# Two-layer hybrid block on one core: the retention branch's gated product goes through DRAM, attention's branch is projected last, and attention's outputs of two units share one PSUM bank

## The chip, the cores and the metric

The kernel runs on one core of one Trainium2 chip, in one launch. The metric is device time in microseconds. The kernel before the change took 2956.39 us (median of 3 runs, 2952.46 to 2957.08).

## The reference

Two layers work on 1024 latent tokens and 256 context tokens of width 1024. Each layer normalises, projects with one wide matrix, runs three token mixers on parts of the projection, gates each mixer's output with its own part of `z` and `g`, and adds the result back:

```
h = rms_norm(x) * (1 + scale) + shift
na, gla, ret, z, g = split(h @ w_in)
o[0] = neighbourhood_attention(na)      # windows of 8 x 16 on a 16 x 64 grid, plus all context tokens
o[1] = gated_linear_attention(gla)      # chunked, both directions
o[2] = retention(ret)                   # chunked, both directions
y = sum_i sigmoid(g[i]) * ((o[i] * silu(z[i])) @ w_branch[i])
x = x + gate * (y @ w_out)
```

`gate`, `shift` and `scale` come from a conditioning vector through `w_mod`. In the last layer only the latent tokens are put out.

## The kernel before

A Python driver writes out the whole order of the program ahead of time. It goes in slots: in each slot the stream of large matrix products (the GEMM stream, line L376) puts in two portions of 3072 moving columns, the workers are advanced twice, and the lane (`attention_lane`) once. `drv.mult` scales the portion, so a larger value spreads the mixers over more GEMM work. Every engine then runs its own list in order and waits on semaphores.

Each GEMM keeps a high and a low part of both operands in fp32r: a unit of `fm_unit` is 24 products of 128x128 weights with up to 512 tokens, a merge unit 12. Layer 0 has 1280 tokens in blocks of 512, 512 and 256, layer 1 has 1024 in two blocks. The stream's order in a layer is: projections for retention, GLA and attention, then 12 groups of `g`, then six groups of `z` (256 columns each, two units of 128 rows per block) in the order `Z_ORDER`, then the merge with branches in the order 2, 1, 0, then the product with `w_out`. `z` groups 0 and 1 belong to attention (branch 0), 2 and 3 to GLA (branch 1), 4 and 5 to retention (branch 2).

The lane runs retention, GLA and attention one after another beside that stream. In attention (`na`), a unit is 128 query tokens of two heads. Each unit is a worker: it loads `q`, `qz`, the bias `bt` and the values `vw`; scores on TensorE (`na_sw`, `na_sc`); softmax on VectorE and ScalarE (`soft1`, `soft2`); ten transposes (`na_ptw`, `na_ptc`) that are copied out as `PT`; then ten products into `na_o` (L1037), which ScalarE copies into `oN`. A new unit starts every three slots. There are 10 units for each of four head pairs in layer 0 and 8 in layer 1. When a head pair has written its outputs, `na_out` is counted up.

A `z` unit's evacuation (`z_evac`) loads the mixer's output `ot`, takes silu on ScalarE and VectorE (L1259, L1260), and multiplies. For branches 0 and 1 GpSimd multiplies (L1273) and SP stores the product to DRAM (`b<-st_z`); `load_b` reads it back in the merge as `rb` and splits it in high and low (L1312, L1313). For branch 2 the product is split at once into resident tiles `bact[2]` in the pool `E`. That pool takes the memory that attention frees, so the lane opens it only after attention has ended; then the lane computes `gate` (`mod_gate`, eight loads of `wt` with products `mod_ps`), and in layer 0 the next layer's shift and scale (`mod_ss`, 16 more).

`z` groups 0 and 1 wait until attention's outputs are written: `while d.get("na_out", 0) < 2 * (zi + 1) * per_pair: yield`. While the stream waits, slots go on without GEMM. All loads go through SP's queue, which starts a load only when its buffer is free and waits there in order. The 8 buffers of `stg` are shared by the evacuations.

Of the kernel before, what the change touches and what calls it, by code (L numbers as in the profile page):

```python
# [30 lines left out]
NCOL = (24, 32, 32, 24)  # L31
LD_LAG, LD_GAP = 3, 3
RT_M = 1.25
GL_M = (1.1, 1.1, 1.0)
GL_N = 13
NA_M1 = 0.7
BR_ORDER = (2, 1, 0)
Z_ORDER = (2, 3, 0, 1, 4, 5)


def _next_f(c):
# [67 lines left out]
def hybrid_kernel(ctx: ExitStack, tc: tile.TileContext, A: dict, out: bass.AP):  # L109
# [777 lines left out]
    def na(layer):  # L887
        d = L[layer]
        ntok, last = d["ntok"], d["last"]
        with tc.tile_pool(name=f"na{layer}", bufs=2) as pn:  # L890
# [21 lines left out]
            def load_v(p):  # L912
# [2 lines left out]
                dma(vcx, d["nv"][NLAT:NTOK, p * P:(p + 1) * P].rearrange("(c p) d -> p c d", p=P))  # L915
                yield

            def heads(p):
                (ks, kl), vcx = tiles["k", p], tiles["v", p]

# [55 lines left out]
                def load_vw(win):  # L976
                    half, j = win
                    cw = 4 * NCOL[j]
                    vw = pn.tile([P, 3, P], F32, tag="vw", name="vw", bufs=4)
                    dma(vw[0:cw], d["nv"][0:NLAT, p * P:(p + 1) * P].rearrange("(g c r) d -> (c r) g d", g=4, r=4)  # L980
                        [4 * COL0[j]:4 * COL0[j] + cw, half:half + 3, :])
                    return vw

                def evac_t(hd, pts, win, vw):
                    hs = slice(hd * 64, hd * 64 + 64)
                    ptw, ptc = pts
                    PT = pn.tile([P, 640], F32, tag="PT", name="PT", bufs=3)
                    ch = []
                    if win is not None:
                        half, j = win  # L990
                        cw = 4 * NCOL[j]
                        ve.tensor_copy(PT[0:cw, 0:384], ptw[0:cw, 0:384])
                        for i in range(3):
                            ch.append((vw[0:cw, i, hs], PT[0:cw, i * P:(i + 1) * P]))
                    sc.copy(PT[:, 384:640], ptc[:, 0:256])
                    for i in range(2):
                        ch.append((vcx[:, i, hs], PT[:, 384 + i * P:384 + (i + 1) * P]))
                    return ch

                def pair(qc, win, dst, after):  # L1000
                    q = pn.tile([P, 2, P], F32R, tag="q", name="q", bufs=3)
# [24 lines left out]
                    for _ in range(5):  # L1026
                        yield
                    ptc = psa("na_ptc", (P, 2, 2 * P))
                    ts = [transp(ps_[hd][0], win, ptc[:, hd]) for hd in range(2)]
                    yield  # L1030
                    cA, cB = [evac_t(hd, ts[hd], win, vw) for hd in range(2)]
                    yield
                    po = psa("na_o")
                    n = len(cA)
                    for i in range(n):
                        for hd, ch in ((0, cA), (1, cB)):
                            pe.matmul(po[64 * hd:64 * hd + 64, 0:P], ch[i][0], ch[i][1], start=i == 0, stop=i == n - 1)  # L1037
                    yield
                    pv = po[:, 0:P]
                    sc.copy(dst, pv.rearrange("d (r c) -> d r c", c=16) if win is not None else pv)  # L1040
                    if after is not None:
                        drv.defer(after)

                for half in range(2):
                    oN = stg("oN")
# [71 lines left out]
    def projections(layer):  # L1117
# [32 lines left out]
                    ga.done = True  # L1150
            gb.done = True

        def fm(g, ns, evac, by_block=False):
            need(g)
            units = [(m, t0, nn) for m in range(g.w // P) for t0, nn in blocks(ns[m])]
            if by_block:
                units.sort(key=lambda u: u[1])
            for m, t0, nn in units:
                yield from fm_unit(g, m, h, t0, nn, evac)
# [92 lines left out]
        def z_evac(zi):  # L1252
            def f(m, t0, nn, ps):
# [8 lines left out]
                def w():  # L1262
                    yield
                    yield
                    if br == 2:
                        bt = d["bact"][2]
                        ve.tensor_tensor(st[:, :nn], st[:, :nn], ot[:, :nn], op=ALU.mult)
                        hi, lo = bt.get(0, ro // P, t0, nn), bt.get(1, ro // P, t0, nn)
                        sc.copy(hi, st[:, :nn])
                        gp.tensor_tensor(lo, st[:, :nn], fv(hi), op=ALU.subtract)  # L1270
                        d["z_out"][t0] = d["z_out"].get(t0, 0) + 1
                    else:
                        gp.tensor_tensor(st[:, :nn], st[:, :nn], ot[:, :nn], op=ALU.mult)  # L1273
                        drv.defer(lambda: dma(d["b"][br][ro:ro + P, t0:t0 + nn], st[:, :nn]))
                drv.spawn(w())
            return f

        per_pair = 2 if last else 3
        d["z_out"] = {}
        for zi in Z_ORDER:  # L1280
            if zi < 2:
                while d.get("na_out", 0) < 2 * (zi + 1) * per_pair:
                    yield
            if zi == 0:
                d["want_E"] = True
            if zi == 4:
                while not d.get("E"):
                    yield
            yield from fm(G["z"][zi], [ntok] * 2, z_evac(zi), zi == 5)
        d["done"]["z"] = True  # L1290


    def merge(layer):
# [7 lines left out]
        def load_b(br):  # L1301
            pend = []
            for t0, nn in blocks(ntok) + [(None, 0)]:
                for k in range(4 if t0 is not None else 2):
                    if t0 is not None:
                        rb = stg("rb")
                        dma(rb[:, :nn], d["b"][br][k * P:(k + 1) * P, t0:t0 + nn])
                        pend.append((rb, k, t0, nn))
                    if len(pend) > 2 or t0 is None:
                        rb_, k_, u0, un = pend.pop(0)  # L1310
                        hi, lo = bact[br].get(0, k_, u0, un), bact[br].get(1, k_, u0, un)
                        sc.copy(hi, rb_[:, :un])  # L1312
                        ve.tensor_tensor(lo, rb_[:, :un], fv(hi), op=ALU.subtract)  # L1313
                    yield
                    yield

        def unit(g, br, bi, m, t0, nn):
            mt = m
# [32 lines left out]
            if end_unit():  # L1351
                yield

        w1 = drv.spawn(load_b(1))
        for bi, br in enumerate(BR_ORDER[:2]):
            if bi == 1:
                while not w1["done"]:
                    yield
                bact[0] = Act(f"bn{layer}", [Ep] * 5, 4, ntok)
                w1 = drv.spawn(load_b(0))  # L1360
            for mg in range(4):
                g = G["wb"][br][mg]
                need(g)
                for m in range(2):
                    for t0, nn in blocks(ntok):
                        while d["z_out"].get(t0, 0) < 4:
                            yield
# [46 lines left out]
    def attention_lane(layer):  # L1414
        d = L[layer]
        for key, fn in (("ret", retention), ("gla", gla), ("nqk", na)):
# [2 lines left out]
            yield  # L1419
            yield  # L1420
            yield from fn(layer)
        while not d.get("want_E"):
            yield
# [5 lines left out]
        d["E"] = E  # L1429
        gate_sb = pgb.tile([98, 256], F32, tag="gate_sb", name="gate_sb")  # L1430
        d["gbc"] = [pgb.tile([P, D], F32, tag=f"gb{v}", name=f"gb{v}") for v in range(1 if d["last"] else 2)]
        with tc.tile_pool(name=f"modw{layer}", bufs=2) as pmw, tc.tile_pool(name=f"modp{layer}", bufs=1) as pm:
# [221 lines left out]
```

## Time and profile before

| | |
|---|---|
| median of 3 runs | 2956.39 us |
| profiled execution | 2953.91 us |
| its span | 2952.1 us |
| TensorE busy | 2828.3 us (96% of the span) |
| VectorE, ScalarE, GpSimd busy | 1499.4, 1102.1, 1078.2 us |
| mean granted TensorE clock | 0.985 |

The profiled execution took 2.48 us less than the median. TensorE is busy nearly all the time, so what counts is where it idles. "Busy" of TensorE holds modelled ends of pipelined products; the idle time that the views give ahead of an instruction is the safer number.

### The profile page before, as it was taken

What the parts mean: (1) busy time and instruction counts of PE and PEld (TensorE: products, weight loads), DVE (VectorE), ACT (ScalarE), POOL (GpSimd) and SP (SyncE); (2) the same over time, 40 slices, a digit from 0 to 9 for tenths busy, and PEclk for the clock granted to TensorE, in tenths of its full rate; (3) what the DMA queues carried; (4) which work ended last, traced back from release to release, by engine and by line L of the source; (5) the groups of instructions that cost most, each with busy time, mean ns of one, the idle gap of its engine ahead of it and who ended that gap; (6) DMA issues with size and microseconds to landing.
All of it is one profiled execution on the core that took longest, in us unless ns stands there. A gap on an engine that the chain in (4) does not pass through costs nothing. (4 is left out here: it accounts for less than half of the span.)

```text
span 2952.1 us, 51923 instructions
## 1 busy us (share of the span) xinstructions
PE 2828.3 (96%) x19776; PEld 2433.6 (82%) x19776; DVE 1499.4 (51%) x3189; ACT 1102.1 (37%) x2569; POOL 1078.2 (37%) x1010
## 2 busy tenths in 40 slices
PE   7999999999999998899999999999999999879999
PEld 5999987788878887677899999987788788767889
DVE  5156567767514455424334346469766156562331
ACT  4133556554423434322113323456544244342110
POOL 4222125466411122043655332125665212204463
PEclk8999999999999999999999999999999999999999
DMA  6344433443244556467445354443433455645543
GB/s 239 107 142 130 139 105 111 115 133 104 92 144 135 170 151 189 125 199 233 136 126 149 104 166 119 132 121 109 145 111 111 148 160 182 181 125 164 183 129 108
DMA packets 390857, 418.69 MB, mean 142 GB/s; under 512 B 33788, under 2 KB 310284, under 8 KB 390608
## 3 DMA queue, kind: packets, MB, share of 16 engines
q1 hardware_dynamic: 353248, 361.59, 40.9%
q10 hardware_dynamic: 37360, 53.79, 5.2%
q8 instruction: 156, 2.56, 0.4%
q14 instruction: 93, 0.76, 0.1%
HBM read 302.72 MB, written 112.54 MB: 141 GB/s over the span
## 5 line engine op out<-in xcount | busy, mean ns | idle before, releaser
L376 PE MATMUL fm<-h,whi 128*128 128x512 f32 (+1 forms) x3936 | 922.6, 380 | 7.7 <-ACT st_g L1244 7.7
L345 POOL TENSOR_TENSOR wlo<-wraw,whi 128x512 fp32r<-128x512 f32 (+1 forms) x336 | 450.5, 1362 | 1000.4 <-ACT whi L342 892.0
L376 PEld LDWEIGHTS fm<-h,whi 128*128 128x128 f32 x3936 | 681.1, 190 | 157.8 <-issue 26.4
L376 PE MATMUL fm<-h,wlo 128*128 128x512 f32 (+1 forms) x1968 | 470.6, 374 | 0.0
L376 PEld LDWEIGHTS fm<-h,wlo 128*128 128x128 f32 x1968 | 339.8, 189 | 70.8 <-issue 8.7
L376 PE MATMUL tm<-whi,h 128*128 128x256 f32 (+1 forms) x2528 | 339.2, 284 | 2.0 <-ACT h L295 2.0
L376 PEld LDWEIGHTS tm<-whi,h 128*128 128x128 f32 x2528 | 318.2, 189 | 3.5 <-ACT h L295 2.7
L342 ACT CAST whi<-wraw 128x1024 fp32r<-128x1024 f32 (+1 forms) x168 | 175.8, 1048 | 268.4 <-PE tm L376 123.8
L376 PE MATMUL tm<-wlo,h 128*128 128x256 f32 (+1 forms) x1264 | 189.7, 286 | 0.0
L376 PEld LDWEIGHTS tm<-wlo,h 128*128 128x128 f32 x1264 | 166.6, 189 | 0.7 <-issue 0.2
L843 DVE TENSOR_TENSOR ek<-dd,kd 128x512 f32<-128x512 f32 x108 | 101.2, 937 | 93.4 <-ACT dd L833 93.2
L376 PE MATMUL tm<-whi,yy 128*128 128x256 f32 x1152 | 147.4, 280 | 0.0
L376 PEld LDWEIGHTS tm<-whi,yy 128*128 128x128 f32 x1152 | 140.7, 188 | 0.1
L1273 POOL TENSOR_TENSOR st_z<-st_z,ot 128x512 f32<-128x512 f32 (+1 forms) x40 | 48.2, 1209 | 253.1 <-DMA ot<-o 103.7
L798 POOL TENSOR_TENSOR dd<-Ac,ash 128x256 f32<-128x256 f32 x126 | 116.3, 923 | 51.5 <-ACT ash L785 31.0
L1260 DVE SCALAR_TENSOR_TENSOR st_z<-st_z,fm 128x512 f32<-128x512 f32 (+1 forms) x60 | 37.8, 633 | 174.4 <-ACT st_z L1259 172.5
L844 DVE SCALAR_TENSOR_TENSOR eq<-dd,g_col,qd 128x256 f32<-128x256 f32 x126 | 117.5, 933 | 13.1 <-ACT dd L833 13.0
L1244 ACT ACTIVATE st_g<-fm 128x512 f32<-128x512 f32 (+1 forms) x120 | 66.5, 557 | 144.0 <-PE fm L376 95.7
L1392 DVE TENSOR_TENSOR st_o<-tm,gb 128x256 f32<-128x256 f32 x72 | 30.5, 424 | 155.1 <-PE tm L376 152.0
L1334 DVE SCALAR_TENSOR_TENSOR gt<-gt,mg 128x512 f32<-128x512 f32 (+1 forms) x80 | 50.7, 634 | 112.5 <-PE mg L376 98.7
L833 ACT ACTIVATE dd<-dd 128x512 f32<-128x512 f32 x126 | 79.4, 635 | 75.3 <-POOL dd L799 73.1
L416 DVE COPY st_tm<-tm 128x256 f32<-128x256 f32 (+1 forms) x59 | 25.2, 428 | 161.5 <-PE tm L376 161.1
(1573 smaller groups left out, 4757.8 us busy)
## 6 DMA issues: line engine op xcount, KB each, us to landing
wraw<-in_w_in SPq DMA_DIRECT2D x104, 512.0 KB
wt<-in_w_mod SPq DMA_DIRECT2D x48, 512.0 KB
gd<-st_g ACTq DMA_DIRECT2D x96, 256.0 KB
gt<-gd SPq DMA_DIRECT2D x96, 256.0 KB
bt<-in_na_bm SPq DMA_DIRECT2D x32, 384.0 KB
ot<-o SPq DMA_DIRECT2D x48, 256.0 KB
wraw<-in_w_branch SPq DMA_DIRECT2D x24, 512.0 KB
v<-ret SPq DMA_DIRECT2D x38, 256.0 KB
```

Of the source, the lines that this page charges most:

```text
L342: sc.copy(hi[:, :, :w], raw[:, :, :w])
L345: gp.tensor_tensor(lo[:, ks, :w], raw[:, ks, :w], fv(hi[:, ks, :w]), op=ALU.subtract)
L376: pe.matmul(ps, a(k), b(k), start=i == 0, stop=i == tot - 1)
L798: gp.tensor_tensor(dv[:, :, Lh:], av[:, :, Lh:], rv, op=ALU.subtract)
L833: sc.activation(E_, E_, AF.Exp)
L843: ve.tensor_tensor(ek_, E_, kd_, op=ALU.mult)
L844: ve.scalar_tensor_tensor(eq[:, :, Lh:], ev[:, :, Lh:], rsc, qv[:, :, Lh:], op0=ALU.mult, op1=ALU.mult)
L1244: sc.activation(st[:, :nn], ps, AF.Tanh, scale=0.5)
L1260: ve.scalar_tensor_tensor(st[:, :nn], st[:, :nn], 1.0, ps, op0=ALU.add, op1=ALU.mult)
L1273: gp.tensor_tensor(st[:, :nn], st[:, :nn], ot[:, :nn], op=ALU.mult)
L1334: ve.scalar_tensor_tensor(gt[:, :nn], gt[:, :nn], 1.0, ps[:, :nn], op0=ALU.add, op1=ALU.mult)
L1392: ve.tensor_tensor(st[:, :256], ps, gbc[0 if t < LT else 1][:, 256 * gi:256 * gi + 256], op=ALU.mult)
```

## The change

The order of the `z` groups becomes GLA, retention, attention. Each half of an attention group now waits for its own head pair only. The retention branch goes the way of the other two: GpSimd multiplies, SP stores to DRAM, and `load_b(layer, 2)` reads it back, started by the lane once attention has ended and pool `E` is open; the merge begins when that has been written into the program. In attention, a unit that has its `PT` tiles is held until the next one has its own, then the products of both go into one PSUM bank. Three factors change: `GL_M[2]` from 1.0 to 1.1, `NA_M1` from 0.7 to 0.8; and three buffer counts: `vw` 4 to 3, `PT` 3 to 4, `q` 3 to 2.

```diff
-GL_M = (1.1, 1.1, 1.0)
+GL_M = (1.1, 1.1, 1.1)
-NA_M1 = 0.7
+NA_M1 = 0.8
-Z_ORDER = (2, 3, 0, 1, 4, 5)
+Z_ORDER = (2, 3, 4, 5, 0, 1)
...
-                    po = psa("na_o")
-                    n = len(cA)
-                    for i in range(n):
-                        for hd, ch in ((0, cA), (1, cB)):
-                            pe.matmul(po[64 * hd:64 * hd + 64, 0:P], ch[i][0], ch[i][1], start=i == 0, stop=i == n - 1)
+                    held.append((cA, cB, dst, after, win))
+                    if len(held) < 2:
+                        return
+                    both_ = list(held)
+                    held.clear()
+                    po = psa("na_o", (P, 2, P))
+                    for u, (cA, cB, _, _, _) in enumerate(both_):
+                        n = len(cA)
+                        for i in range(n):
+                            for hd, ch in ((0, cA), (1, cB)):
+                                pe.matmul(po[64 * hd:64 * hd + 64, u, :], ch[i][0], ch[i][1], start=i == 0, stop=i == n - 1)
...
-                    if br == 2:
-                        bt = d["bact"][2]
-                        ve.tensor_tensor(st[:, :nn], st[:, :nn], ot[:, :nn], op=ALU.mult)
-                        hi, lo = bt.get(0, ro // P, t0, nn), bt.get(1, ro // P, t0, nn)
-                        sc.copy(hi, st[:, :nn])
-                        gp.tensor_tensor(lo, st[:, :nn], fv(hi), op=ALU.subtract)
-                        d["z_out"][t0] = d["z_out"].get(t0, 0) + 1
-                    else:
-                        gp.tensor_tensor(st[:, :nn], st[:, :nn], ot[:, :nn], op=ALU.mult)
-                        drv.defer(lambda: dma(d["b"][br][ro:ro + P, t0:t0 + nn], st[:, :nn]))
+                    gp.tensor_tensor(st[:, :nn], st[:, :nn], ot[:, :nn], op=ALU.mult)
+                    drv.defer(lambda: dma(d["b"][br][ro:ro + P, t0:t0 + nn], st[:, :nn]))
...
             if zi < 2:
-                while d.get("na_out", 0) < 2 * (zi + 1) * per_pair:
-                    yield
...
+                def wait(m, zi=zi):
+                    return d.get("na_out", 0) >= (2 * zi + m + 1) * per_pair
+            yield from fm(G["z"][zi], [ntok] * 2, z_evac(zi), wait)
...
+        while not d.get("b2") or not d["b2"]["done"]:
+            yield
```

How the order changes on TensorE at the end of attention in layer 1. The names: `na_ptw`, `na_ptc` are one unit's transposes, `na_sw`, `na_sc` one unit's scores, `fm` is the `z` product that waited, `mod_ps` the product for `gate`. Before, the last unit but one and the last, then GEMM:

```order
L928 MATMUL na_sc<-k_26492,q 128x256
L929 MATMUL na_sc<-kl,qz_24369 128x256
L971 MATMUL na_ptw<-ident,P__27594 128x128 x3
L973 MATMUL na_ptc<-ident,P__27594 128x128 x2
L971 MATMUL na_ptw<-ident,P__27601 128x128 x3
L973 MATMUL na_ptc<-ident,P__27601 128x128 x2
L1037 MATMUL na_o<-PT,vw 64x128 x6
L1037 MATMUL na_o<-PT,vcx 64x128 x4
L971 MATMUL na_ptw<-ident,P__27658 96x128 x3
L973 MATMUL na_ptc<-ident,P__27658 128x128 x2
```

Now, the last two units of the same layer:

```order
L931 MATMUL na_sc<-kl,qz_24504 128x256
L973 MATMUL na_ptw<-ident,P__27932 128x128 x3
L975 MATMUL na_ptc<-ident,P__27932 128x128 x2
L973 MATMUL na_ptw<-ident,P__27939 128x128 x3
L975 MATMUL na_ptc<-ident,P__27939 128x128 x2
L973 MATMUL na_ptw<-ident,P__28007 96x128 x3
L975 MATMUL na_ptc<-ident,P__28007 128x128 x2
L973 MATMUL na_ptw<-ident,P__28014 96x128 x3
L975 MATMUL na_ptc<-ident,P__28014 128x128 x2
L1045 MATMUL na_o<-PT,vw 64x128 x6
L1045 MATMUL na_o<-PT,vcx 64x128 x4
L1045 MATMUL na_o<-PT,vw 64x128 x6
```

The products `na_o` of one unit no longer stand behind that unit's transposes, but behind the next one's, and the transposes of the last unit (`P__28007`) stand close behind the scores they come from.

On SP behind the end of attention in layer 0. Before, the loads `wt` of `mod_gate` and `mod_ss` lie between the `ot` loads of retention's `z` units:

```order
L116 DMA wt<-in_w_mod 128x1024
L116 DMA ot<-o_0_95 128x512
L116 DMA wt<-in_w_mod 128x1024 x2
L116 DMA ot<-o_0_95 128x512
L116 DMA wraw_13787<-in_w_branch 128x4x256
L116 DMA wt<-in_w_mod 128x1024 x2
```

Now the read-back of retention's branch (`rb<-b_0_98`) lies between the `wt` loads of `mod_gate`:

```order
L116 DMA rb<-b_0_98 128x512
L116 DMA wt<-in_w_mod 128x1024
L116 DMA rb<-b_0_98 128x512 x2
L116 DMA wt<-in_w_mod 128x1024
L116 DMA rb<-b_0_98 128x512 x2
L116 DMA wt<-in_w_mod 128x1024
L116 DMA rb<-b_0_98 128x512 x2
L116 DMA wt<-in_w_mod 128x1024
```

Twelve loads of 256 or 128 KB have come in there in layer 0, and eight in layer 1, each pair behind a `wt` load that waits for its buffer.

## Rows read from the trace of the kernel before

**Rows 1.** The page: busy time of each engine, and TensorE's share and granted clock in 40 equal slices of the span (digits are tenths).

```profile
PE 2828.3 (96%) x19776; PEld 2433.6 (82%) x19776; DVE 1499.4 (51%) x3189; ACT 1102.1 (37%) x2569; POOL 1078.2 (37%) x1010
...
PE   7999999999999998899999999999999999879999
```

**Rows 2.** Busy time by stretch, at the end of attention in layer 0 (from 1160) and in layer 1 (from 2560): length, PE, PEld, DVE, ACT, POOL busy with instruction counts, granted clock, DMA share, GB/s.

```profile
1160.00:1180.00 20.00, 13.57 (x90) 11.32 (x92) 14.50 (x48) 11.18 (x37) 7.07 (x6) 0.83 0.69 203
...
2560.00:2580.00 20.00, 9.94 (x70) 8.57 (x67) 6.43 (x19) 4.92 (x14) 5.04 (x4) 0.74 0.74 217
2580.00:2600.00 20.00, 14.79 (x120) 12.17 (x119) 14.12 (x49) 9.99 (x34) 2.80 (x2) 0.92 0.56 162
```

**Rows 3.** Waits of PE from 1150 to 1245 us, and then from 2540 to 2700 us: who was waited for, us in total, times, longest.

```profile
PE na_o L1037 <- DVE PT L992: 9.5, 7, 1.5
PE na_o L1037 <- ACT PT L995: 8.1, 4, 3.1
PE mod_ps L210 <- DMA wt<-in_w_mod: 1.5, 1, 1.5
PE na_o L1037 <- issue: 1.4, 1, 1.4
...
PE na_o L1037 <- DVE PT L992: 24.8, 11, 10.1
PE mod_ps L210 <- DMA wt<-in_w_mod: 2.7, 1, 2.7
PE na_o L1037 <- ACT PT L995: 0.6, 1, 0.6
```

**Rows 4.** PE in order of time, one round of a unit in layer 1's tail: start, length, instruction, in brackets the idle time ahead and its releaser.

```profile
2589.55 1.22 PE L1037 MATMUL na_o<-PT,vw 128*64 128x128 f32 x11 [1.50 <-DVE PT L992]
...
2591.32 0.40 PE L928 MATMUL na_sw<-k,q 128*128 128x288 f32 x1
...
2592.45 0.49 PE L971 MATMUL na_ptw<-ident,P__27099 128*96 128x128 f32 x3
...
2593.32 0.38 PE L973 MATMUL na_ptc<-ident,P__27106 128*128 128x128 f32 x2
2595.20 1.22 PE L1037 MATMUL na_o<-PT,vw 96*64 96x128 f32 x11 [1.50 <-DVE PT L992]
```

**Rows 5.** The softmax of one unit in the tail: its last score on PE, and on DVE its last scaling, behind another unit's copies `PT`.

```profile
2580.02 0.28 PE L929 MATMUL na_sc<-kl,qz 128*128 128x256 f32 x1
...
2582.29 1.01 DVE L992 COPY PT<-na_ptw 128x384 f32<-128x384 f32 x2
...
2584.46 0.55 DVE L962 TENSOR_SCALAR P__27025<-P__27025,nst 128x640 f32<-128x640 f32 x1
```

**Rows 6.** A wait of one context unit in layer 0's drain (PE), and the longest wait of layer 1's tail: PE, the ACT instruction behind it, and SP's queue ahead of it (what SP waited for, us, times, longest, from 2530 to 2600).

```profile
1218.38 1.39 PE L1037 MATMUL na_o<-PT,vcx 128*64 128x128 f32 x8 [2.44 <-ACT PT L995]
...
2575.45 1.79 PE L1037 MATMUL na_o<-PT,vw 96*64 96x128 f32 x11 [10.06 <-DVE PT L992]
...
2573.61 0.60 ACT L1259 ACTIVATE st_z<-fm 128x512 f32<-128x512 f32 x1 [6.03 <-DMA b<-st_z]
...
SPq L116 <- POOL st_z L1273: 11.2, 2, 10.4
```

**Rows 7.** PE in steady attention of layer 1: GEMM, one unit's products, GEMM, the next scores.

```profile
2546.75 2.58 PE L376 MATMUL fm<-h,whi 128*128 128x512 f32 x10
2549.26 0.88 PE L1037 MATMUL na_o<-PT,vw 128*64 128x128 f32 x12
2549.96 0.61 PE L1037 MATMUL na_o<-PT,vcx 128*64 128x128 f32 x8
2550.50 1.42 PE L376 MATMUL fm<-h,whi 128*128 128x512 f32 x5
2551.76 0.29 PE L928 MATMUL na_sw<-k,q 128*128 128x288 f32 x1
```

**Rows 8.** By stretch as in rows 2: a stretch in layer 0's merge in which the loads `wt`, `rb` and `gt` run together; and attention beside GLA's `z` units in layer 0 and layer 1.

```profile
1325.00:1345.00 20.00, 20.00 (x130) 13.74 (x130) 8.54 (x14) 4.98 (x8) 4.01 (x4) 1.00 0.95 323
...
1060.00:1140.00 80.00, 79.24 (x540) 67.54 (x539) 50.30 (x128) 32.67 (x101) 22.46 (x19) 1.00 0.65 194
...
2460.00:2560.00 100.00, 100.00 (x646) 82.64 (x646) 66.04 (x169) 42.77 (x127) 28.80 (x22) 1.00 0.58 176
```

**Rows 9.** PE behind the tail of layer 0, in order of time, and sizes of loads by line (KB each).

```profile
1226.61 0.61 PE L210 MATMUL mod_ps<-wt,csi 128*2 128x256 f32 x8 [1.48 <-DMA wt<-in_w_mod]
...
1230.13 0.61 PE L210 MATMUL mod_ps<-wt,csi 128*2 128x256 f32 x8
...
wt<-in_w_mod SPq DMA_DIRECT2D x48, 512.0 KB
...
rb<-b SPq DMA_DIRECT2D x32, 256.0 KB
```

**Rows 10.** Other waits of PE: in GLA's second phase of layer 0 (630 to 800 us) and layer 1 (2105 to 2130 us), and over the whole span the merge's wait for retention's tiles.

```profile
PE gla_lv L813 <- DVE eq L845: 4.1, 3, 1.4
...
PE gla_lv L813 <- DVE eq L845: 3.6, 1, 3.6
PE gla_lv L813 <- DVE eq L844: 0.5, 1, 0.5
...
PE mg L376 <- ACT br L1269: 2.1, 1, 2.1
```

More of the change, by code (lines that the diff above doesn't have):

```diff
@@ L916, in load_v @@
                 yield
+            held = []
             def heads(p):
@@ L978, in load_vw @@
                     cw = 4 * NCOL[j]
-                    vw = pn.tile([P, 3, P], F32, tag="vw", name="vw", bufs=4)
+                    vw = pn.tile([P, 3, P], F32, tag="vw", name="vw", bufs=3)
                     dma(vw[0:cw], d["nv"][0:NLAT, p * P:(p + 1) * P].rearrange("(g c r) d -> (c r) g d", g=4, r=4)
@@ L986, in evac_t @@
                     ptw, ptc = pts
-                    PT = pn.tile([P, 640], F32, tag="PT", name="PT", bufs=3)
+                    PT = pn.tile([P, 640], F32, tag="PT", name="PT", bufs=4)
                     ch = []
@@ L1000, in pair @@
                 def pair(qc, win, dst, after):
-                    q = pn.tile([P, 2, P], F32R, tag="q", name="q", bufs=3)
+                    q = pn.tile([P, 2, P], F32R, tag="q", name="q", bufs=2)
                     dma(fv(q[:]), d["nq"][p, :, :, qc:qc + P].rearrange("h d t -> d h t"))
@@ L1032, in pair @@
                     yield
-                    po = psa("na_o")
-                    n = len(cA)
-                    for i in range(n):
-                        for hd, ch in ((0, cA), (1, cB)):
-                            pe.matmul(po[64 * hd:64 * hd + 64, 0:P], ch[i][0], ch[i][1], start=i == 0, stop=i == n - 1)
-                    yield
[L1039 to L1042, printed above, removed]
+                    held.append((cA, cB, dst, after, win))
[9 more added lines that the diff above has]
+                                pe.matmul(po[64 * hd:64 * hd + 64, u, :], ch[i][0], ch[i][1], start=i == 0, stop=i == n - 1)
+                    yield
+                    for u, (_, _, dst, after, win) in enumerate(both_):
+                        pv = po[:, u, :]
+                        sc.copy(dst, pv.rearrange("d (r c) -> d r c", c=16) if win is not None else pv)
+                        if after is not None:
+                            drv.defer(after)
                 for half in range(2):
@@ L1151, in tm2, with fm @@
             gb.done = True
-        def fm(g, ns, evac, by_block=False):
+        def fm(g, ns, evac, wait=None):
             need(g)
[L1155 to L1159, printed above, removed]
+            for m in range(g.w // P):
+                while wait is not None and not wait(m):
+                    yield
+                for t0, nn in blocks(ns[m]):
+                    yield from fm_unit(g, m, h, t0, nn, evac)
             g.done = True
@@ L1278, in projections, with stored, load_b @@
         per_pair = 2 if last else 3
-        d["z_out"] = {}
         for zi in Z_ORDER:
+            wait = None
             if zi < 2:
-                while d.get("na_out", 0) < 2 * (zi + 1) * per_pair:
-                    yield
[L1284 to L1287, printed above, removed]
-                    yield
-            yield from fm(G["z"][zi], [ntok] * 2, z_evac(zi), zi == 5)
-        d["done"]["z"] = True
+                def wait(m, zi=zi):
+                    return d.get("na_out", 0) >= (2 * zi + m + 1) * per_pair
+            yield from fm(G["z"][zi], [ntok] * 2, z_evac(zi), wait)
+            if zi == 5:
+                def stored():
+                    for _ in range(12):
+                        yield
+                    d["want_b2"] = True
+                drv.spawn(stored())
+        d["done"]["z"] = True
+    def load_b(layer, br):
+        d = L[layer]
+        bact, ntok = d["bact"], d["ntok"]
+        pend = []
+        for t0, nn in blocks(ntok) + [(None, 0)]:
+            for k in range(4 if t0 is not None else 2):
+                if t0 is not None:
+                    rb = stg("rb")
+                    dma(rb[:, :nn], d["b"][br][k * P:(k + 1) * P, t0:t0 + nn])
+                    pend.append((rb, k, t0, nn))
+                if len(pend) > 2 or t0 is None:
+                    rb_, k_, u0, un = pend.pop(0)
+                    hi, lo = bact[br].get(0, k_, u0, un), bact[br].get(1, k_, u0, un)
+                    sc.copy(hi, rb_[:, :un])
+                    ve.tensor_tensor(lo, rb_[:, :un], fv(hi), op=ALU.subtract)
+                yield
+                if br < 2:
+                    yield
     def merge(layer):
@@ L1299, in merge @@
         bact[1] = Act(f"bg{layer}", [U] * 5, 4, ntok)
[L1301 to L1315, printed above, removed]
         def unit(g, br, bi, m, t0, nn):
@@ L1352, in unit @@
                 yield
-        w1 = drv.spawn(load_b(1))
+        while not d.get("b2") or not d["b2"]["done"]:
+            yield
+        w1 = drv.spawn(load_b(layer, 1))
         for bi, br in enumerate(BR_ORDER[:2]):
@@ L1359, in merge @@
                 bact[0] = Act(f"bn{layer}", [Ep] * 5, 4, ntok)
-                w1 = drv.spawn(load_b(0))
+                w1 = drv.spawn(load_b(layer, 0))
             for mg in range(4):
@@ L1365, in merge @@
                     for t0, nn in blocks(ntok):
-                        while d["z_out"].get(t0, 0) < 4:
-                            yield
                         yield from unit(g, br, bi, 2 * mg + m, t0, nn)
@@ L1421, in attention_lane @@
             yield from fn(layer)
-        while not d.get("want_E"):
-            yield
         es = d["es"] = ExitStack()
@@ L1429, in attention_lane @@
         d["E"] = E
+        while not d.get("want_b2"):
+            yield
+        d["b2"] = drv.spawn(load_b(layer, 2))
         gate_sb = pgb.tile([98, 256], F32, tag="gate_sb", name="gate_sb")
```

## The prediction, made before the run

> **What bounds the kernel now.** I read the page first. TensorE is busy for 2828.3 us of the span, and its row of 40 slices stays at 9 except at the start and in a few slices [rows 1]. No other engine comes near, so the GEMM stream sets the time, and what a change can give lies in the places where TensorE idles. The table of stretches shows two of them: the ends of attention, from about 1160 us on in layer 0 and from about 2560 us on in layer 1. There TensorE works 9.9 to 14.8 us of each 20, and in some of the stretches below the full clock (granted 0.83 and 0.74) [rows 2].
>
> The reason is in the order. Before, `z` groups 0 and 1 wait for attention's outputs while the stream has nothing else to offer, so the last twelve rounds of attention in each layer run without GEMM between them; I call this the tail. The waits of TensorE say what a tail costs: 9.5 + 8.1 + 1.4 = 19.0 us in layer 0 and 24.8 + 0.6 = 25.4 us in layer 1 in front of `na_o`, 44.4 us together [rows 3]. A round shows the pattern: scores 1.1 us, transposes 1.2 us, then an idle 1.50 us until VectorE has copied `PT`, then the products; from one `na_o` to the next it is 5.65 us [rows 4].
>
> **The change, part by part.** It removes no product of TensorE, so the sum is made of waits alone, against the profiled execution's 2953.9 us.
>
> *Fewer rounds in the tail.* With retention's `z` units ahead of attention's, and larger slots, the new order leaves less attention without GEMM: in layer 0 six units (three bursts of `na_o`), in layer 1 two units (one burst) and a little later six more (three bursts). I priced the new tails from the old rows. Each burst waits for the `PT` of its second unit: 1.50 us, and 2.44 us for the burst of context units, the row of layer 0's drain [rows 4, 6]. New is a second kind of wait. The first unit's products no longer stand between one unit's scores and its own transposes, so the transposes can stand close behind the scores, and they need the whole softmax. The rows give that chain: the last score ends at 2580.30 us, the last scaling at 2585.01 us, 4.7 us [rows 5].
>
> In layer 0 the first such place has 14 GEMM products of 256 columns between (half of the 0.251 us that one of 512 takes [rows 7], so 1.8 us), transposes and scores, 4.1 us in all, and waits 0.6 us; the second has one set of transposes and two context scores, 1.7 us, and waits 3.0 us; the third is a context unit with 0.5 us between. No row shows a context unit's chain alone: its wait lies between 0 and 4.7 - 0.5 = 4.2 us, and I take the middle, 2.1 us, as it has one exponential fewer. With the bursts, 1.5 + 1.5 + 2.4, that makes 11.1 us. In layer 1 the places have enough between them, 2.3 us (wait 2.4) and 1.2 us (wait 3.5), and with four bursts at 1.5 us the sum is 11.9 us. So 44.4 us become 23.0 us: a gain of 21.4 us. This includes the loss of one long wait of 10.06 us, which I come back to.
>
> *PSUM in the tail.* Attention has five banks, and in the new tail transposes, scores and transposes follow each other, nine tiles before the burst. They can wait for copies. No row prices it: between nothing and one pair of `PT` copies, 1.01 us [rows 5], for each of seven bursts, 7 us. I take 3 us, between the ends, since the scores wait for the softmax anyway at three of those places.
>
> *Retention's branch through DRAM.* The arithmetic stays: a multiplication, a copy and a subtraction for each of 20 units move between VectorE and GpSimd. New are 20 stores and 20 loads. The stores lie beside attention, where DMA is 65% and 58% busy while TensorE works 79.24 of 80 us and all of 100 us [rows 8]; I cost them at nothing, with that slack as the cover. The loads lie behind the tail, between the `wt` loads, and the merge's first products wait for them. In layer 0 five slots of GEMM are left then; a slot with a `mod_ps` takes 3.52 us [rows 9], so 17.6 us. In that time 2.6 MB of `rb`, six `wt` of 0.52 MB and about 0.65 MB of `ot` must come, 6.4 MB. The densest stretch of this kernel moved 323 GB/s at a DMA share of 0.95, with TensorE busy all the time [rows 8]; at that rate 6.4 MB take 19.9 us, 2.3 us more than the GEMM covers. In layer 1 it is four slots, 14.1 us, for 4.7 MB, 14.6 us, 0.5 us over. I take 2.8 us; the ends are nothing, if `wt` comes later without harm, and 14.4 us, if none of the 4.65 MB read back is hidden.
>
> The Trainium skill, "DMA: Bandwidth & Descriptors", section "Specifications", puts the limit of a core's HBM traffic near 358 GB/s. The row's 323 GB/s lies under it and agrees with a limit of that order. By the page's figure the same bytes would take 17.9 and 13.1 us, and the term would be 0.3 us in place of 2.8 us.
>
> *What goes with it.* The merge's one wait for retention's tiles, 2.1 us in the old order [rows 10], has no cause left when the tiles are written from `rb` well ahead: a gain of 2.1 us, or nothing. Making two units' outputs in one burst saves 36 changes between GEMM and `na_o`. The rows show such a change as free: 10 products take 2.51 us ahead of one, five take 1.26 us behind it, and 20 halves of `na_o` take 1.24 us [rows 7]. I take 0, at most one such product (0.06 us) a change, 2.2 us. `GL_M[2]` stretches GLA's second phase where TensorE waited for VectorE, 4.1 us in layer 0 and 4.1 us in layer 1 [rows 10]. Ten per cent more GEMM in a slot removes a part: I take 2 us, between 0 and 8.2. Its price, attention starting some seven slots later, is in the tail's count already.
>
> **The sum.** -21.4 + 3 + 2.8 - 2.1 - 0 - 2 = -19.7 us. The profiled execution would come to 2934.2 us. It was 2.5 us below the median; taken from the median, 2956.4 - 19.7 = 2936.7 us. I predict 2937 us.
>
> **Rivals.** *More is won.* Layer 0's tail ran at 0.83 in one stretch and layer 1's at 0.74 and 0.92, between the levels of 1.2 and 2.4 GHz, behind waits of 3.1 and 10.1 us [rows 2, 3]. If the shorter waits leave the clock full, the 13.57, 9.94 and 14.79 us of work there shrink by about 2.3 + 2.6 + 1.2 = 6 us; with GLA's full 8.2 us and no bank waits it is 6 + 6 + 3 = 15 us more: 2922 us. Against it: two of my new waits are 3 us and more.
>
> *Nothing is won.* The 10.06 us wait did not come from the tail's pattern. ScalarE's `st_z` stood behind the store `b<-st_z` of an earlier unit for 6.03 us, and SP had been held for up to 10.4 us at a store whose product GpSimd had not made [rows 6]. What SP holds back then are attention's own loads. It cost 10.06 - 1.50 = 8.6 us, once in 20 `z` units beside attention. Now 40 units with stores stand beside attention. Two such waits give 17 us back: 2954 us. For it speaks that each retention unit now adds a store behind GpSimd; against it, the stretches of rows 8, where GLA's units stood beside attention with almost no idle time.
>
> *Slower.* The same mechanism, but at four places in place of one: SP's queue is held at stores of retention's units whenever GpSimd is behind, and with three `vw` and two `q` buffers the loads of attention have less lead. Four times 8.6 is 34 us, 2937 + 34 = 2971 us. It decides from the third place on, where the gain of 19.7 us is eaten.
>
> **How the numbers follow.** The main case has 0.66, with its own range 2926 to 2948; more is won 0.12; nothing is won 0.14; slower 0.08. The range that should hold eight in ten goes from 2918 to 2956: it takes in the larger gain and the case without one, and leaves out the slower end. What a measurement of this kernel can tell from no change is about 0.2%, 5.9 us. Faster than 2950.5 us are the main case, the larger gain and a little of the third: 0.80. Within 0.2% is most of the third: 0.11. Slower: 0.09.
>
> **What would show it.** In the changed profile the waits in front of `na_o` and of the transposes in the two tails should sum to 20 to 26 us, with bursts that wait 1.5 us and two or three transposes that wait 2 to 4 us on VectorE's scaling. Behind each tail the merge's first products should wait under 3 us for `br`. The waits of `gla_lv` from VectorE should be a little smaller. I am wrong if the tails are as long in idle time as before, if the merge waits 5 us or more for the read-back, or if `st_z` and attention's loads wait behind SP at several places while `z` runs beside attention.

## The result and the profile after

The changed kernel took 2903.40 us (median of 4 runs, 2902.28 to 2906.68), the kernel before in the same comparison 2956.54 us: a ratio of 0.9825, with a 95% interval of 0.9808 to 0.9842. That is 53 us faster. The prediction was 2937 us, with a range from 2918 to 2956 us: the sign was right, the size was not. The profiled execution's span went from 2952.1 to 2901.2 us.

The page of the changed kernel, with the two rows that answer to [rows 1]:

```profile
PE 2805.8 (97%) x19776; PEld 2426.2 (84%) x19776; DVE 1512.9 (52%) x3189; ACT 1095.4 (38%) x2569; POOL 1077.6 (37%) x1010
...
PE   7999999999999999989999999999999989998999
```

The number of TensorE's instructions is the same, and yet its busy time fell from 2828.3 to 2805.8 us, 22.5 us. The rest of the span, in which TensorE idles, fell from 123.8 to 95.4 us, 28.4 us. These two are the 50.9 us by which the span fell. The forecast of 19.7 us had only looked for the second.

Waits of PE in the two tails, as in [rows 3]: from 1150 to 1275 us, and from 2560 to 2700 us (who was waited for, us in total, times, longest).

```profile
PE mod_ps L210 <- DMA wt<-in_w_mod: 2.9, 1, 2.9
PE na_ptc L975 <- DVE P__13629 L964: 2.1, 1, 2.1
PE na_ptw L973 <- DVE nst L962: 2.1, 1, 2.1
PE na_ptw L973 <- DVE P__13358 L964: 1.6, 1, 1.6
PE na_sc L930 <- ACT PT L997: 1.3, 1, 1.3
PE na_ptw L973 <- DVE nst L946: 0.6, 1, 0.6
PE na_ptc L975 <- DVE P__13634 L964: 0.3, 1, 0.3
```

```profile
PE na_sc L930 <- ACT PT L997: 4.7, 2, 4.1
PE na_ptw L973 <- DVE nst L962: 3.2, 2, 2.9
PE mod_ps L210 <- DMA wt<-in_w_mod: 2.5, 1, 2.5
PE na_ptw L973 <- DVE P__27719 L964: 1.6, 1, 1.6
PE na_ptw L973 <- DVE nst L946: 1.4, 3, 0.5
PE na_sw L930 <- DVE PT L994: 0.8, 1, 0.8
PE na_o L1045 <- DVE nst L946: 0.3, 1, 0.3
```

Without `mod_ps` that is 8.0 and 12.0 us, 20.0 us where 44.4 us stood before. In this view, `na_o` waits only once, for 0.3 us.

PE in the tail of layer 1, in order of time: the last pair but one and its transposes, then the last one's (start, length, instruction, idle time ahead and releaser).

```profile
2638.44 0.88 PE L1045 MATMUL na_o<-PT,vw 96*64 96x128 f32 x12 [0.29 <-DVE nst L946]
2639.14 0.61 PE L1045 MATMUL na_o<-PT,vcx 128*64 128x128 f32 x8
2639.79 1.23 PE L1045 MATMUL na_o<-PT,vw 128*64 128x128 f32 x11
...
2642.75 0.49 PE L973 MATMUL na_ptw<-ident,P__27932 128*128 128x128 f32 x3
...
2646.89 0.84 PE L973 MATMUL na_ptw<-ident,P__28007 128*96 128x128 f32 x3 [2.89 <-DVE nst L962]
...
2649.16 1.55 PE L1045 MATMUL na_o<-PT,vw 128*64 128x128 f32 x12
```

The reader sees why the burst hardly waits at its start: its first half uses a unit whose `PT` was copied long ago, and while that runs the copies of the second unit go on. They are not always done in time: here they last until 2641.00 us, and the second half, from 2639.79 us on, still waits inside for them (how, is shown below). The longest wait ahead of an instruction has moved to the transposes (2.89 us), which stand close behind their scores.

### The profile page after: what moved, and what is told of

Same layout as the page of the kernel before. It is cut to its first block, busy times and chain, and to the rows that moved or that the text cites. A ratio compares the mean times of both kernels' runs of the same rounds, so it can differ in the third digit from the quotient of the medians.

```text
span 2901.2 us, 52147 instructions
## 1 busy us (share of the span) xinstructions
PE 2805.8 (97%) x19776; PEld 2426.2 (84%) x19776; DVE 1512.9 (52%) x3189; ACT 1095.4 (38%) x2569; POOL 1077.6 (37%) x1010
## 3 DMA queue, kind: packets, MB, share of 16 engines
q1 hardware_dynamic: 359008, 371.03, 42.4%
## 5 line engine op out<-in xcount | busy, mean ns | idle before, releaser
L1274 POOL TENSOR_TENSOR st_z<-st_z,ot 128x512 f32<-128x512 f32 (+1 forms) x60 | 74.4, 1246 | 254.4 <-DMA ot<-o 115.0
L799 POOL TENSOR_TENSOR dd<-ash,Ac 128x256 f32<-128x256 f32 x126 | 106.6, 846 | 0.0
```

Source lines behind the costliest of these rows:

```text
L799: gp.tensor_tensor(dv[:, :, :Lh], rv, av[:, :, :Lh], op=ALU.subtract)
```

## The experiments

The question was where the 33 us come from that the prediction did not have. Each series of runs has the kernel before beside it, at 2953.5 to 2956.7 us (medians), so kernels of different series are compared by their ratios to it.

**Taking the change apart.** Four runs: the changed kernel with one burst per unit again (e1); the kernel before with pairs and the three buffer counts alone (e2); the changed kernel with the old order (e5); the new order with single bursts and the old factors (e6).

```diff
 # e1: in the changed kernel (e2 is the reverse, in the kernel before)
-                    held.append((cA, cB, dst, after, win))
-                    if len(held) < 2:
-                        return
...
-                    po = psa("na_o", (P, 2, P))
+                    po = psa("na_o")
 # e5
-Z_ORDER = (2, 3, 4, 5, 0, 1)
+Z_ORDER = (2, 3, 0, 1, 4, 5)
 # e6: e1, and
-GL_M = (1.1, 1.1, 1.1)
-NA_M1 = 0.8
+GL_M = (1.1, 1.1, 1.0)
+NA_M1 = 0.7
```

> The changed kernel with each unit's outputs made alone again (one PSUM tile a unit); order, read-back and factors stay. The tails hold as much attention without GEMM as in the changed kernel. Theory A (a round in the tail costs TensorE more than its visible wait: the products run slowly behind it, and pairing also shortens the steady bursts): 10 to 17 us slower than the changed kernel, 2914 to 2920 us, with na_o busy back near 115 us. Theory B (pairing is worth nothing, the order and the factors give everything): 2902 to 2907 us.

Measured: 2922.11 us, ratio 0.9894 (0.9877 to 0.9911), 0.69% or some 20 us of the gain gone. More than either theory had; the pairing is far from worthless.

> The kernel before with the pairing alone (and its buffer counts); z order, resident retention tiles and factors as before, so the tails keep all 24 rounds without GEMM. Theory A: 15 to 25 us faster than before, 2931 to 2941 us, since 24 waits of 1.5 us become 12 waits for softmax and na_o in the tail runs faster. Theory B: 2951 to 2957 us.

Measured: 2934.38 us, 0.9934 (0.9919 to 0.9948). Pairs alone give 19 us in the old order.

> The changed kernel with the old z order (attention's groups third, retention's last), still through DRAM and paired. By the order written into the program the tails hold 690 instructions without GEMM in place of 320. If a tail's cost goes with its length (both theories): some 28 us slower than the changed kernel, 2925 to 2935 us. If the read-back from DRAM is itself dear where nothing covers it: 2940 us and more, with a wait of 10 us or more in front of the merge's first products.

Measured: 2978.96 us, 1.0085 (1.0070 to 1.0100): slower than before. Waits of PE behind layer 0's attention, from 1285 to 1335 us:

```profile
PE mod_ps L210 <- DMA rb<-b: 11.7, 1, 11.7
PE mod_ps L210 <- DMA wt<-in_w_mod: 8.7, 5, 2.9
```

When retention's `z` units come last, nothing is left to cover their read-back. The waits of `mod_ps` ahead of the two merges come to 39.8 us; in the changed kernel they are 5.5 us. (The longest one of layer 1, 13.3 us, has no releaser in the view; SP issues the first `rb` and `wt` there only behind the last stores of retention's units.) The read-back is cheap in the changed kernel because attention's `z` units stand beside it.

> The order and the read-back alone: no pairing, GL_M[2] 1.0 and NA_M1 0.7 as before. By the written order only 96 instructions of attention are left without GEMM, in layer 1. Theory A with the tail's whole cost (44 us of waits and some 15 us hidden in slow products) removed with it: 40 to 52 us faster than before, 2905 to 2916 us. If the factors and the pairing are what made the order pay: 2930 us or more.

Measured: 2914.55 us, 0.9867 (0.9850 to 0.9883), 39 us better than before. Order and pairs, 39 and 19 us alone, come to 58 us, more than the changed kernel's 53 us; it also has the two larger factors, which are tried below (e7).

**Where the pairs gain.** In e9 only the last head pair of a layer, at whose end the tails stand, makes pairs; in e10 only the first three.

```diff
-                    if len(held) < 2:
+                    if p == 3 and len(held) < 2:
```

(`p < 3` in e10.)

> The changed kernel, with outputs of two units in one burst only for the last head pair of each layer (the one whose end has no GEMM beside it); the first three head pairs make one burst per unit. All singles took 2922 us, all in pairs 2903 us. Tail theory (the 19 us of the pairing lie where no GEMM runs beside attention: a single burst waits there for PT and its products run slowly behind the wait): nearly all of the gain stays, 2903 to 2908 us. Uniform theory (each change between GEMM and a burst costs something everywhere, so the gain goes with the number of bursts, and three quarters of them are single again): about 2903 + 14 = 2917 us.

Measured: 2919.25 us, 0.9877 (0.9863 to 0.9891).

> The mirror of the run with pairs in the last head pair only: outputs in pairs for the first three head pairs of each layer, where GEMM runs beside attention, single bursts for the last. Tail theory: the waits in front of na_o come back to about 26 us as with all singles, and the time to 2917 to 2922 us. Uniform theory: only a quarter of the gain goes, about 2903 + 5 = 2908 us, and the total busy time of na_o stays near 105 to 107 us.

Measured: 2912.08 us, 0.9854 (0.9840 to 0.9868). Against all singles (0.9894), pairs in the last head pair bring 0.17% or 5 us, pairs in the first three 0.40% or 12 us. The uniform theory was nearer in both, and the theory I had begun with, that the tails hold the gain, fell. The intervals of e1 and e9 overlap, so the 5 us are not certain by themselves.

The trace shows a cost. PE in steady attention of layer 0, in the run with singles (e1) and then in the changed kernel, at the same place of the program:

```profile
911.34 2.11 PE L376 MATMUL fm<-h,whi 128*128 128x512 f32 x8
913.29 0.63 PE L376 MATMUL fm<-h,wlo 128*128 128x512 f32 x2
913.86 0.88 PE L1039 MATMUL na_o<-PT,vw 128*64 128x128 f32 x12
914.56 0.61 PE L1039 MATMUL na_o<-PT,vcx 128*64 128x128 f32 x8
915.10 1.42 PE L376 MATMUL fm<-h,wlo 128*128 128x512 f32 x5
916.36 0.29 PE L930 MATMUL na_sw<-k,q 128*128 128x288 f32 x1
```

```profile
909.28 2.12 PE L376 MATMUL fm<-h,whi 128*128 128x512 f32 x8
911.23 1.77 PE L376 MATMUL fm<-h,wlo 128*128 128x512 f32 x7
912.85 0.30 PE L930 MATMUL na_sw<-k,q 128*128 128x288 f32 x1
```

The same 15 GEMM products take 2.52 + 1.26 = 3.78 us with the burst between them and 3.57 us without, 0.21 us less, with no wait in either. The burst itself takes 1.24 us for 20 products (the trace records each of a unit's ten instructions as two) and 2.34 us for 40, so a pair saves another 0.14 us. Together 0.35 us for each burst that goes. Over 16 units of layer 0 in which neither kernel idles, from the first context score of unit 15 to that of unit 31, the changed kernel needs 159.1 us (1026.53 to 1185.67) and the one with singles 162.0 us (1029.78 to 1191.78): 2.9 us for eight pairs, 0.36 us each. These two stretches, in the view of [rows 2], e1 first:

```profile
1029.78:1191.78 162.00, 162.00 (x1098) 137.16 (x1097) 97.46 (x248) 62.83 (x192) 47.98 (x40) 1.00 0.56 171
1026.53:1185.67 159.14, 159.14 (x1097) 137.90 (x1097) 99.33 (x252) 61.88 (x192) 48.03 (x41) 1.00 0.58 176
```

Of the changed kernel's 36 bursts 29 stand beside GEMM, 29 x 0.36 = 10.4 us; with 7.5 us less waiting in attention (19.3 against 26.8 us, gaps of 0.3 us and more) that is 17.9 of the 18.9 us between the two spans.

**The factors, and the tails.** Each of these is the changed kernel with other values: e3 `GL_M[2]` 1.0; e4 `NA_M1` 0.7; e7 both; e11 `NA_M1` 0.65; e8 1.0 and 0.65; e12 is e11 with singles, by the edit of e1.

> The changed kernel with the factor GL_M[2] back at 1.0: GLA takes fewer slots, attention starts earlier, and fewer of TensorE's instructions at the end of attention have no GEMM beside them (50 and 96, against 120, 48 and 152). Tail theory: shorter tails decide, 2893 to 2900 us, with waits of na_ptw, na_sc and na_o there down by 8 us or more. Theory that the larger slot pays in GLA's second phase: its waits there come back (about 4 us) and the time stays at 2903 or rises, to 2910 us.

Measured: 2899.28 us, 0.9807 (0.9794 to 0.9821). The waits of GLA are back as in [rows 10] (4.1 us from 630 to 800 us), attention's fell by 3 us, not 8, and the time did not rise: what the factor gives in GLA it takes elsewhere. Against the changed kernel the difference is within the intervals.

> The changed kernel with the factor NA_M1 back at 0.7. The instructions without GEMM fall only in layer 0 (92 against 120). Tail theory: 2899 to 2903 us, a gain of one round at most. Theory that a larger slot relieves attention beside GEMM (fewer waits for its loads): waits of fm and na_ptw in the steady part of layer 1 grow, 2905 to 2912 us.

Measured: 2895.51 us, 0.9795 (0.9782 to 0.9808), better than both theories had it. The gain lies in layer 0 alone, as the count of instructions in the tail does: the rest of the program, from layer 0's merge on, runs 10 us ahead of the changed kernel's.

> The changed kernel with both factors as before (GL_M[2] 1.0, NA_M1 0.7): the run with the order alone (2914.6 us), plus pairs. Almost no tail is left (96 instructions, in layer 1). Switch theory (each change between GEMM and a burst of na_o costs TensorE about 0.18 us, so 36 pairs save about 13 us beside GEMM, as unit starts of the changed kernel and of the one with singles show: 159.1 against 162.0 us for eight pairs without an idle moment): 2897 to 2902 us. Tail theory: only the two bursts of the short tail gain, 2908 to 2912 us.

Measured: 2896.65 us, 0.9798 (0.9784 to 0.9813), some 20 us below e6 by pairs alone, with hardly a tail. The switch theory was the nearer one, but its 36 x 0.36 = 13 us are not all: 3 us more are idle gaps (85.0 against 87.7 us), and the rest stays open. By the ratios e7 also lies some 8 us below the changed kernel: the two larger factors, which the change brought in, seem to cost time (the two intervals just touch).

> The changed kernel with NA_M1 0.65: a portion of GEMM in attention is four products of 512 columns in place of five in layer 1 (eight or nine of 256 in place of ten in layer 0), and attention ends with GEMM still beside it: no tail. If the tails' cost can be taken back (20.0 us of waits, and bursts behind waits of 3.0 to 3.5 us against 2.34 us beside GEMM, 5 us): 2876 to 2886 us. Rival: with less GEMM beside a unit its loads, softmax and copies are no longer covered and waits appear beside GEMM in place of the tails': 2893 us or more.

Measured: 2882.94 us, 0.9755 (0.9740 to 0.9769). The tails' cost can be taken back; the rival that waits come up beside GEMM did not come.

> The same kernel with NA_M1 0.65 and no tail, but one burst per unit. Switch theory: 36 more bursts beside GEMM cost 11 to 15 us against the run with pairs. Tail theory (the pairs' gain comes from rounds without GEMM): there are none, so 0 to 3 us.

Measured: 2911.18 us, 0.9852 (0.9836 to 0.9869), 28 us above the one with pairs: more than either theory. Its waits of PE, in attention of layer 0 (870 to 1250 us) and of layer 1 (2340 to 2660 us):

```profile
PE na_o L1039 <- ACT PT L997: 5.0, 3, 2.3
PE na_o L1039 <- DVE PT L994: 1.1, 3, 0.7
...
PE na_o L1039 <- ACT PT L997: 6.9, 3, 3.7
```

With smaller portions of GEMM a single burst waits for `PT` beside GEMM too. Attention's waits (again gaps of 0.3 us and more) are 14.7 us here against 4.4 us with pairs, 10.3 us more; with 36 x 0.36 = 13.0 us that is 23 of the 28 us, and 5 us stay open.

> GL_M[2] 1.0 and NA_M1 0.65 with pairs: no tail either, and GLA takes fewer slots. If GL_M[2] 1.1 only pays in GLA's waits, 3 to 5 us above the run with 1.1 and 0.65; if less GEMM in GLA and more beside attention is better in itself, equal or below it.

Measured: 2874.17 us, 0.9724 (0.9709 to 0.9738): faster than both kernels, 30 us below the changed one by the ratios. The last 20 us of attention in each layer, in the view of [rows 2], and TensorE's row of slices:

```profile
1195.00:1215.00 20.00, 20.00 (x151) 16.91 (x150) 7.07 (x18) 6.64 (x19) 6.50 (x6) 1.00 0.22 71
2590.00:2610.00 20.00, 19.92 (x158) 16.59 (x158) 12.80 (x29) 6.42 (x21) 6.56 (x5) 1.00 0.39 122
```

```profile
PE   7999999899999999999999999999999999999999
```

PE is full and the clock at its upper level of 2.4 GHz (granted 1.00). `GL_M[2]` 1.1 is worth nothing here: with 1.0 the time is 9 us below e11. The idle gaps account for 3.4 us of it (65.8 against 69.2 us); the rest stays open.

**What a change of shape costs.** Open was whether any short burst costs 0.36 us or only one of another shape. In the rows `na_o` has 128*64 where the GEMM has 128*128. In e14 (on e12) and e13 (on e8) each product takes the values of both heads as weights and writes 128 rows, of which a copy takes the half that is wanted: as many products and moving columns, one more copy per unit on ScalarE, and 128 rows of output throughout. The order changes with it: one head's products now stand behind the other's, where they alternated.

```diff
-                            ch.append((vw[0:cw, i, hs], PT[0:cw, i * P:(i + 1) * P]))
+                            ch.append((vw[0:cw, i, :], PT[0:cw, i * P:(i + 1) * P]))
...
-                        for i in range(n):
-                            for hd, ch in ((0, cA), (1, cB)):
-                                pe.matmul(po[64 * hd:64 * hd + 64, u, :], ch[i][0], ch[i][1], start=i == 0, stop=i == n - 1)
+                        for hd, ch in ((0, cA), (1, cB)):
+                            for i in range(n):
+                                pe.matmul(po[:, u, hd, :], ch[i][0], ch[i][1], start=i == 0, stop=i == n - 1)
```

> The kernel with NA_M1 0.65 and one burst per unit (2911.2 us), with na_o in products of 128 output rows in place of 64: each head's product takes the weights of both heads' values (128x128 in place of 128x64), writes its own 128 columns of the bank, and two copies of 64 rows take out the half that is wanted. As many products with as many moving columns. Shape theory (a change between products of 128x128 and 128x64 costs TensorE time, a change among 128x128 forms none): the 72 bursts lose about 0.22 us each, 0.15 in the GEMM ahead and 0.10 behind against 0.03 where only transposes and scores change: 2895 us or less. Burst theory (any short burst between GEMM costs this, whatever its shape): 2908 to 2915 us, as before.

Measured: 2941.47 us, 0.9953 (0.9936 to 0.9969).

> The same edit to the fastest version so far (pairs, GL_M[2] 1.0, NA_M1 0.65, 2874.2 us): 36 bursts. Shape theory: 36 times 0.22 us less, 2864 to 2868 us. Burst theory: 2872 to 2878 us.

Measured: 2930.12 us, 0.9913 (0.9898 to 0.9928). Both are slower, by 30 and 56 us, which neither theory had. One burst of a pair in e13, and one in e8:

```profile
902.78 0.83 PE L1045 MATMUL na_o<-PT,vw 128*128 128x128 f32 x6
...
907.16 0.71 PE L376 MATMUL fm<-h,wlo 128*128 128x512 f32 x2
```

```profile
902.63 0.88 PE L1045 MATMUL na_o<-PT,vw 128*64 128x128 f32 x12
...
904.97 0.74 PE L376 MATMUL fm<-h,wlo 128*128 128x512 f32 x2
```

Forty products take 4.38 us in the full shape and 2.34 us in halves: two heads' products run beside each other in the half shape, and I had not seen that. But the rows answer the question as well. In the full shape 20 products take 2.15 us and 40 take 4.38 us, so a burst has no fixed cost; in the half shape 1.24 and 2.34 us leave 0.14 us (2 x 1.24 - 2.34). And the GEMM runs around a burst, against 0.235 us a product (the median of long runs), have 0.06 us too much ahead and 0.07 us behind in e13, where e8 has 0.17 and 0.10 us. The times agree: with NA_M1 0.65, single bursts take 28 us more than pairs in the half shape (e12 and e11). In the full shape e14 lies 11 us above e13, of which `GL_M[2]` is worth 9 us (e11 and e8), so about 2 to 3 us are left, with several us of uncertainty. So most of the cost goes with the half shape, as the shape theory says, while its forecast of the time was wrong. Whether it is the shape itself or the alternation of the two heads, which went with it, was not tried apart. The Trainium skill, "TensorEngine Tiling (Array Packing)", section "Tiling Modes", states that a change of the tiling mode drains TensorE and that tiles of one mode work independently; these rows agree with both.

## Why the prediction was right or wrong

*What bounds the kernel: right.* The gaps of TensorE at the ends of attention held the largest term, and no other engine became the bound.

*Fewer rounds in the tail: right in the sum, not in its parts.* 44.4 us became 20.0 us, where the forecast had 23.0 us and 3 us for banks. The step "each burst waits for the `PT` of its second unit: 1.50 us" failed: seven bursts wait 0.3 us together at their start, since the first unit's products cover all or most of the second one's copies. The waits of transposes for the softmax, forecast at 0.6, 3.0 and 2.1 us in layer 0 and 2.4 and 3.5 us in layer 1, came as 2.2, 2.1 and 2.4 us and as 1.6 and 2.9 us. PSUM cost more than the 3 us taken: 1.3 us in layer 0, 4.7 + 0.8 us in layer 1, within the bound of 7. Of that, 4.1 us are one wait, which stands again under the rivals.

*"It removes no product of TensorE, so the sum is made of waits alone": the step that failed.* 22.5 us of the gain are in busy time. `na_o` fell by 14.9 us (119.9 to 105.0) and the products `fm` of 512 columns by 7.8 us. Two causes can be sized. Beside GEMM 29 bursts stand where 48 stood, 19 x 0.36 = 6.8 us. And in the old tail a burst was slow as well as late: rows of the kernel before, one burst there from its start to the next scores, with the weight loads ahead of its third and later products on `vw` (PEld), the copies that it needs (DVE, ACT), and the stretches around it.

```profile
2608.17 1.23 PE L1037 MATMUL na_o<-PT,vw 128*64 128x128 f32 x11 [1.50 <-DVE PT L992]
...
2610.01 0.40 PE L928 MATMUL na_sw<-k,q 128*128 128x288 f32 x1
...
2608.63 0.63 PEld L1037 LDWEIGHTS na_o<-PT,vw 128*64 128x64 f32 x10 [0.28 <-DVE PT L992]
...
2607.56 1.01 DVE L992 COPY PT<-na_ptw 128x384 f32<-128x384 f32 x2
...
2608.75 0.63 ACT L995 COPY PT<-na_ptc 128x256 f32<-128x256 f32 x2
```

```profile
2605.00:2610.00 5.00, 3.46 (x35) 2.74 (x33) 4.31 (x16) 2.85 (x10) 0.00 (x0) 1.00 0.40 115
2610.00:2615.00 5.00, 3.46 (x33) 2.95 (x32) 3.98 (x14) 2.96 (x11) 0.00 (x0) 1.00 0.37 106
```

It takes 1.84 us at the full clock, where [rows 7] have 1.24 us. [rows 4] showed it too: 1.77 us from 2589.55 to 2591.32. The burst starts when the first head's copy on VectorE is made, but the second head's lasts until 2608.57 us, and the third product's weights wait 0.28 us for it. ScalarE's copies last until 2609.38 us, and the last products on `vcx` need them. All 20 such bursts of the old tails have VectorE's second copy ending 0.37 to 0.51 us into the burst. As the ends of the products are modelled, the view of PE counts these inner waits as busy. Over the 24 bursts of the old tails the time above that of a burst beside GEMM sums to 15.4 us, over the six slow ones of the new tails to 5.9 us: 9.5 us. The stretches at the lower clock of 1.2 GHz make some 4 us of the first sum and 5 us of the second, so what fell are the inner waits, from about 11 to 1 us. The other 6.2 us of busy time stay open. So the step of the forecast that failed is its list of terms: it had nothing for busy time, where the profile lost 22.5 us.

*"I take 0" for the pairs: wrong, and in the reading.* The products of 0.251 us in [rows 7] were my measure for an undisturbed product. They stand right beside the bursts, and so held the cost that I looked for; a long run has 0.235 us. The bound of 2.2 us came from the same measure. A burst taken out gives 0.36 us, of which 0.21 us are in the GEMM around it.

*Read-back, 2.8 us: about right.* The merge waited 1.5 us (for VectorE's `y`, not for `rb`), the `wt` loads 5.5 us in place of 4.2 us. *The wait for `br`, -2.1 us:* gone, and the 1.5 us stand in its place. *`GL_M[2]`, -2 us:* 4.1 us became 0.9 us in layer 0 and stayed 4.1 us in layer 1, and e3 shows no gain from the factor in sum. Not seen was a longer wait at the start of layer 1's attention, in the changed kernel:

```profile
2331.12 1.22 PE L376 MATMUL fm<-h,whi 128*128 128x512 f32 x2 [10.15 <-ACT whi L342]
```

Before, the wait of that place was 4.42 us, so 5.7 us were lost there; it is about 10 us in e4 and e11 too, and about 5 us in e3 and e8, which have the old `GL_M[2]`: the factor brought it. At the start of layer 0's attention the same factor took a wait of 3.3 us down to 1.1 us.

*The rivals.* Nothing won, and slower, rested on SP being held at stores. It was held: 56.3 us in layer 0's attention and 40.1 us in layer 1's, longest 10.3 us (before: 42.4 and 29.1 us, longest 15.6 us). The only wait of TensorE that may follow from it is the one of 4.1 us for `PT`, where ScalarE's `st_z` had waited 6.91 us for the load `ot`; there was no second. More won had the right direction, but its cause, the clock, is not what the runs show for most of it: the new tails still have 0.83 (1230 to 1250 us) and 0.91 (2560 to 2580 us). The mean granted clock of the profiled execution did rise, from 0.985 to 0.991, but much of that lies at the start of the program (20 to 45 us: 0.59 before, 1.00 now), where TensorE mostly waits for loads and both kernels are level again at 62 us.

## What to carry to other kernels

Rows beside an event are no measure of what the event costs: take the undisturbed rate from a long run elsewhere, and compare the same instructions with and without the event between them. When instructions of another tile shape are strewn into a GEMM stream, gather them: the gain goes with the number of changes, not with the number of products. And when a wait is to go, look also at how slowly the work behind it runs, and for what it waits inside, since "busy" hides that.

## What was not expected of the hardware

A burst of 128*64 products between 128*128 ones cost 0.36 us beside its own work, an estimated 13 us over 36 bursts. Two heads' products in 64 columns each ran in 58 ns apiece (2.34 us / 40) where full products with as many moving columns took 110 ns (4.38 us / 40). A burst that started on the first of its copies took 1.84 us in place of 1.24 us at full granted clock, and the view of PE showed the 0.6 us between as busy.
